# Value projection of a two-mixer decoder layer: two of its four token tiles swap PSUM banks

## The chip, the cores and the metric

The kernel runs on one core of one Trainium2 chip. The metric is device time in microseconds (us), the median of several executions. Beside it there is a trace of one profiled execution.

## The reference

One decoder layer over 1024 tokens of width 1024, in float32. A normalised input is projected eight ways; one part goes through a gated linear recurrence (RG-LRU), another through a chunked linear attention with a decaying state (HGRN2, 8 heads of width 128); gates merge both, an output projection and a residual follow, then an MLP and a last norm:

```python
proj = h @ w_in
xa, ga, q, f, v, g, m_a, m_b = jnp.split(proj, SPLIT_POINTS, axis=-1)
xa = causal_depthwise_conv(xa, conv_w, conv_b)
y_a = rg_lru(xa, w_r, b_r, w_i, b_i, lam) * jax.nn.gelu(ga)
...
o = rms_norm(hgrn2_chunkwise(qf, kf, log_f, vf), hg_norm)
y_b = o * jax.nn.silu(g)
y = jax.nn.sigmoid(m_a) * y_a + jax.nn.sigmoid(m_b) * y_b
x = x + y @ w_out
x = x + jnp.square(jax.nn.relu(rms_norm(x, norm_mlp) @ w_up)) @ w_down
return rms_norm(x, norm_final)
```

The change touches only the part `v`, the values of the linear attention.

## The kernel before

**Numbers.** Each float32 operand is split into a high part, which is a rounded copy (`split`, a ScalarE CAST at L87), and a low part, which is the rest (a VectorE subtraction at L88). Each product is then three TensorE matmuls (`mm3`, L144 to L146).

**Stages.** The mixers are worked in eight stages: 2 halves of 512 tokens (`c`) by 4 pairs of heads (`p`), stage `i` being `c, p = divmod(i, 4)`. A stage is a Python generator that yields after every few matmuls. `hgrn` for stage `i` runs on VectorE, ScalarE and GpSimd, and calls `go(n)`, which advances the generator of stage `i + 1` by `n` steps; so the projections of the next stage fill TensorE while the attention of this one is prepared. A last generator, `last_stage`, follows the eighth stage. TensorE's order is pinned to the order in which the code is written from the first stage on; the other engines' order is set by a scheduler with priorities.

**What one stage puts on TensorE, in order** (`stage`, from `i` = 2 on): the value projection of the stage before (`v_of(i)`, which calls `v_steps` for `i - 1`), the projections `xa` and `q`, most of `f`, the four gate products of the recurrence (`rg_lru`: `pr` and `pi` for `s` = 0 and `s` = 1), and the rest of `f`. Between them lie, at the places that `hgrn` chooses, the score blocks of the attention (`blocks`, L570, and the lines L690 and L701), the transposes `pk`, and the products `pkv` and `po`.

**The value projection.** `v_steps` works on four token tiles `tt` of 128 tokens. Each is a group of 24 matmuls of 256 columns into a PSUM bank of its own (tile names `pv_..._0` to `pv_..._3` in the order, `pv` in the trace), which ScalarE then copies to SBUF (L427). After the second tile (`tt` = 1; after the third in stage 2) `on_T` puts eight transposes of the previous attention's output on TensorE (`poT`, L438) into banks of another group.

**Banks.** There are eight PSUM banks in three groups (`bank`): four tagged `pj`, two `sc`, two `hg`. A new tile takes, in its group, the bank whose earlier tile is used up first in the program's order, and the first matmul into it waits for the last reader of that earlier tile. In a stage the `pj` tiles are three of the value tiles, two each of `xa`, `q` and `f`, and `pr`, `pi` for `s` = 0; the `sc` tiles are one value tile, `pr`, `pi` for `s` = 1, two score blocks and one later block of the attention (`sc64`). In the `pj` group `pr` and `pi` are opened after the two `f` tiles but are used up before them. So the value tiles that come next take the banks of `pr`, `pi`, and then of the first `f` tile, in that order.

**Who reads the `f` tiles.** `f_of` reads each of the two `f` tiles twice on ScalarE: a sigmoid into `f` (L550) and one into `kk` (L551). They stand behind `normalised` (L784, eight small ACTIVATEs that scale the attention's output) in ScalarE's queue.

Of the kernel before, what the change touches and what calls it, by code (L numbers as in the profile page):

```python
# [45 lines left out]
def trunk(ctx: ExitStack, tc: tile.TileContext, x, wts, mlp, pv, gains, mask_f, mask_u, out):  # L46
# [15 lines left out]
    def bank(tag, name):  # L62
        return ps.tile([P, 512], F32, tag=tag, name=name, bufs={"pj": 4, "sc": 2, "hg": 2}[tag])
# [68 lines left out]
    def next_w():  # L132
        used[0] += 1
        return get_w(used[0] - 1)
# [7 lines left out]
    def mm3(o, ah, al, bh, bl, first, last, goes_on=False):  # L142
        how = {"skip_group_check": True} if goes_on else {}
        pin(PE.matmul(o, ah, bh, start=first, stop=False, **how))  # L144
        pin(PE.matmul(o, ah, bl, start=False, stop=False, **how))  # L145
        pin(PE.matmul(o, al, bh, start=False, stop=last, **how))  # L146
# [49 lines left out]
    def kt(set_, k):  # L196
        return set_[0][k // 4][:, k % 4, :], set_[1][k // 4][:, k % 4, :]
# [20 lines left out]
    def mt(tag, name, shape=(P, T), dt=F32, bufs=1):  # L218
        return m.tile(list(shape), dt, tag=tag, name=name, bufs=bufs)
# [193 lines left out]
    def v_steps(c, p, got, between):  # L413
        v = mt("v", f"v_{c}{p}", (P, 4, 256))
        w = [next_w(), next_w()]
        for tt in range(4):
            pp = bank("pj" if tt < 3 else "sc", f"pv_{c}{p}_{tt}")
            for k in range(8):
                hh, hl = kt(hT[c], k)
                cut = slice(tt * P, (tt + 1) * P)  # L420
                cols = slice((k % 4) * 256, (k % 4 + 1) * 256)
                wh, wl = w[k // 4]
                mm3(pp[:, :256], hh[:, cut], hl[:, cut], wh[:, cols], wl[:, cols], k == 0, k == 7)
                if k % 2:
                    if k < 7:
                        yield
            A.copy(v[:, tt, :], pp[:, :256])  # L427
            between(tt)
            yield
        got["v"] = v  # L430
# [375 lines left out]
    def v_of(i):  # L806
        def between(tt):
            if tt == 0:
                gots[i - 1]["tail"]()
            if tt == (2 if i == 2 else 1):  # L810
                on_T(*where(i - 2), gots[i - 2])
            for n in {}.get((i, tt), ()):
                with tc.high_priority(400):
                    transposed(xn1[n], hT[1], n, f"x1{n}")

        yield from v_steps(*where(i - 1), gots[i - 1], between)

    def stage(i):
        c, p = where(i)
        got = gots[i]  # L820
        if i == 0:
            yield from v_steps(c, p, got, lambda tt: None)
        elif i > 1:
            yield from v_of(i)
# [516 lines left out]
    for part in range(2):  # L1341
# [4 lines left out]
        for hf in range(2):  # L1346
            pp = {tt: bank("pj", f"po1{hf}{tt}") for tt in tts}
# [184 lines left out]
    for kb in range(n_kb):  # L1532
        last = kb + 1 == n_kb
        qs = order[2 * kb : 2 * kb + 2]
        for half in range(2):
# [8 lines left out]
            for step, (bk, wo, uo), prs in [  # L1544
# [11 lines left out]
                for pr in prs:  # L1556
                    _, ci, cj, op = ADDS[step]
# [92 lines left out]
```

## Time and profile before

| what | value |
|---|---|
| median of 3 executions | 1545.02 us (1544.61 to 1545.60) |
| the profiled execution: from its first to its last instruction | 1544.2 us |
| busy share of that span: TensorE matmul, its weight loads, VectorE, ScalarE, GpSimd | 99%, 83%, 74%, 52%, 10% |
| mean granted TensorE clock | 0.998 of full speed |

The profiled execution's own time outside its span isn't told by the trace; the span stands 0.8 us under the median. In the trace, PE is TensorE's matmuls, PEld its weight loads, DVE is VectorE, ACT ScalarE, POOL GpSimd. A row of the chain in time gives the start in us, the duration in us, the engine, the line, the operation with output and input, and in square brackets how long the engine had stood idle before it and what ended that. The last transposes of the mixers (`poT`) start at 559.5 us; the gates, the output projection and the MLP follow.

### The profile page before, as it was taken

How to read it: one execution, taken by the hardware profiler on the slowest of the kernel's cores; microseconds unless marked ns; L12 is line 12 of the kernel's file. 1: busy time of each engine (PE TensorE's matmuls, PEld its weight loads, DVE VectorE, ACT ScalarE, POOL GpSimd, SP SyncE). 2: the span in 40 equal slices, each digit the busy share in tenths (PEclk: the TensorE clock that was granted, in tenths of full speed). 3: DMA queues.
4: the chain of work that ended last, by engine and by line, in shares of the span. 5: the costliest groups of instructions: out<-in, count | busy, mean ns of one | idle time of the engine just before them, and what ended most of it. 6: DMA issues, size and time to landing. Idle time of an engine off the chain costs nothing. (4 is left out here: it accounts for less than half of the span.)

```text
span 1544.2 us, 23190 instructions
## 1 busy us (share of the span) xinstructions
PE 1527.6 (99%) x9081; PEld 1275.3 (83%) x9081; DVE 1150.0 (74%) x1656; ACT 810.2 (52%) x1341; POOL 149.8 (10%) x188
## 2 busy tenths in 40 slices
PE   8999999999999999999999999999999999999998
PEld 7878888888888887888888888888888788888886
DVE  5798595485675928786866568888788898888877
ACT  5647757568567435453533347766666721111115
POOL 1021210233515600000000000000000000000000
PEclk9999999999999999999999999999999999999999
DMA  7555455465664274432328323666666675666642
GB/s 285 188 173 192 151 190 182 151 218 172 236 212 158 96 286 164 164 135 84 137 94 314 151 109 143 267 247 246 244 249 248 228 312 224 249 252 250 252 186 109
DMA packets 81679, 306.82 MB, mean 199 GB/s; under 512 B 8481, under 2 KB 20897, under 8 KB 68642
## 3 DMA queue, kind: packets, MB, share of 16 engines
q1 hardware_dynamic: 77536, 292.75, 51.8%
q10 hardware_dynamic: 4034, 12.59, 2.1%
q8 instruction: 71, 1.16, 0.3%
q14 instruction: 38, 0.31, 0.1%
HBM read 201.50 MB, written 103.81 MB: 198 GB/s over the span
## 5 line engine op out<-in xcount | busy, mean ns | idle before, releaser
L1559 DVE TENSOR_TENSOR acc<-acc,dX 128x512 f32<-128x512 f32 x128 | 85.0, 683 | 28.6 <-PE dX L146 26.9
L87 ACT CAST wA<-q 128x512 fp32r<-128x512 f32 x46 | 28.6, 622 | 147.5 <-PE dX L146 101.7
L88 DVE TENSOR_TENSOR wL<-raw,wH 128x1024 fp32r<-128x1024 f32 x48 | 58.8, 1225 | 46.0 <-ACT wH L87 45.7
L87 ACT CAST wH<-raw 128x1024 fp32r<-128x1024 f32 x48 | 50.4, 1050 | 39.4 <-DMA raw<-wts_in 16.1
L1559 DVE TENSOR_TENSOR acc<-acc,dY 128x512 f32<-128x512 f32 x64 | 43.4, 685 | 13.1 <-PE dY L146 12.9
L144 PE MATMUL po<-wH,y 128*128 128x512 f32 x128 | 49.8, 393 | 0.0
L145 PE MATMUL po<-wL,y 128*128 128x512 f32 x128 | 49.8, 389 | 0.0
L146 PE MATMUL po<-wH,y 128*128 128x512 f32 x128 | 49.7, 390 | 0.0
L1420 ACT ACTIVATE b<-b 128x512 f32<-128x512 f32 x48 | 30.2, 630 | 32.2 <-DVE b L1419 32.0
L88 DVE TENSOR_TENSOR wA<-q,wA 128x512 fp32r<-128x512 f32 x46 | 31.5, 686 | 16.6 <-ACT wA L87 16.4
L108 ACT CAST wH<-raw 128x1024 fp32r<-128x1024 f32 x36 | 37.7, 1048 | 9.8 <-issue 3.7
L465 DVE SCALAR_TENSOR_TENSOR xc<-xp,pvt,xc 128x512 f32<-128x512 f32 x48 | 40.1, 846 | 1.1 <-ACT xc L449 1.1
L171 POOL TENSOR_TENSOR rstd_h<-rstd_h,mhalf 128x1 f32<-128x1 f32 x8 | 4.6, 584 | 371.9 <-DVE rstd_h L166 371.9
L981 DVE TENSOR_TENSOR s<-q,q 128x512 f32<-128x512 f32 x46 | 31.6, 686 | 4.4 <-DMA q<-mlp_in 4.0
L378 POOL TENSOR_TENSOR stt<-r,stt 128x256 fp32r<-128x256 f32 x16 | 19.9, 1261 | 127.6 <-ACT stt L377 115.4
L989 DVE TENSOR_TENSOR s<-q 128x512 f32<-128x512 f32 x46 | 31.6, 686 | 0.4
L1421 ACT ACTIVATE b<-b 128x512 f32<-128x512 f32 x48 | 30.2, 631 | 1.2
L769 ACT ACTIVATE on<-po 128x128 f32<-128x128 f32 x64 | 16.9, 278 | 26.1 <-PE po L765 26.0
L1071 DVE TENSOR_TENSOR gb<-gY,ge 128x512 f32<-128x512 f32 x14 | 9.7, 690 | 25.1 <-PE gY L146 25.1
L146 PEld LDWEIGHTS po<-wH,y 128*128 128x128 f32 x128 | 24.0, 188 | 5.1
L145 PEld LDWEIGHTS po<-wL,y 128*128 128x128 f32 x128 | 24.1, 188 | 4.8
L144 PEld LDWEIGHTS po<-wH,y 128*128 128x128 f32 x128 | 24.0, 188 | 4.7
(2546 smaller groups left out, 5448.9 us busy)
## 6 DMA issues: line engine op xcount, KB each, us to landing
q<-mlp_in SPq DMA_DIRECT2D x92, 512.0 KB, 3.8
raw<-wts_in SPq DMA_DIRECT2D x80, 512.0 KB, 4.9
rest<-wL SPq DMA_DIRECT2D x36, 512.0 KB, 2.9
wL<-rest SPq DMA_DIRECT2D x36, 512.0 KB, 4.2
hd<-ri SPq DMA_DIRECT2D x16, 256.0 KB, 3.7
od<-onT ACTq DMA_DIRECT2D x8, 512.0 KB, 7.3
cdT<-stT SPq DMA_DIRECT2D x16, 256.0 KB, 3.4
o<-od SPq DMA_DIRECT2D x4, 1024.0 KB, 6.8
```

The costliest lines, as they stand in the source:

```text
L87: keep(A.copy(h, src))
L88: ins = V.tensor_tensor(out=lo, in0=src, in1=h.bitcast(F32), op=ALU.subtract)
L108: A.copy(h, raw)
L144: pin(PE.matmul(o, ah, bh, start=first, stop=False, **how))
L145: pin(PE.matmul(o, ah, bl, start=False, stop=False, **how))
L146: pin(PE.matmul(o, al, bh, start=False, stop=last, **how))
L465: ins = V.scalar_tensor_tensor(xc[:, s, :], xp[:, j : j + T], pvt[:, PV_CW + 8 * j + u : PV_CW + 8 * j + u + 1], xc[:, s, :], op0=ALU.mult ...
L981: ins = V.tensor_tensor(out=sa[:, 0, :], in0=a21, in1=a22, op=ALU.add)
L989: V.tensor_tensor(out=sb[:, 0, :], in0=a21, in1=a11, op=ALU.add)
L1420: A.activation(b[:, at, :], b[:, at, :], AF.Relu, scale=-1.0 if at == 2 else 1.0)
L1421: A.activation(b[:, at, :], b[:, at, :], AF.Square)
L1559: V.tensor_tensor(out=dst, in0=dst, in1=banks[bk, pr], op=op)
```

## The change

The third token tile (`tt` = 2) takes the bank from the `sc` group instead of the fourth one (`tt` = 3), in all eight calls of `v_steps`:

```diff
         for tt in range(4):
-            pp = bank("pj" if tt < 3 else "sc", f"pv_{c}{p}_{tt}")
+            pp = bank("sc" if tt == 2 else "pj", f"pv_{c}{p}_{tt}")
             for k in range(8):
```

The number of tiles from each group stays the same. Every engine has the same instructions in the same order before and after; what moves are the waits of three TensorE instructions in a stage. The first two places are TensorE's in stage 5, where the values of the fifth attention are projected (`poT` are the transposes of `on_T`, `pv_2` and `pv_3` the third and fourth token tile, `Activation_49` a wait for a ScalarE instruction):

```order
 L438 MATMUL poT_3498<-ident,on_3179 128x128 x3
-L144 MATMUL pv_2_3505<-wH_3288,hT10H 128x256 [waits Activation_49]
+L144 MATMUL pv_2_3505<-wH_3288,hT10H 128x256
 L145 MATMUL pv_2_3505<-wL_3289,hT10H 128x256
 L146 MATMUL pv_2_3505<-wH_3288,hT10L 128x256
@@ -1472,5 +1471,5 @@
 L145 MATMUL pv_2_3505<-wL_3310,hT11H 128x256
 L146 MATMUL pv_2_3505<-wH_3309,hT11L 128x256
-L144 MATMUL pv_3_3531<-wH_3288,hT10H 128x256
+L144 MATMUL pv_3_3531<-wH_3288,hT10H 128x256 [waits Activation_49]
 L145 MATMUL pv_3_3531<-wL_3289,hT10H 128x256
```

The wait on ScalarE moves from the first matmul of the third tile to the first matmul of the fourth, 24 matmuls later. The third place is the second bank of the `q` projection (`pj_q_1`) of the same stage, also on TensorE:

```order
 L145 MATMUL pj_q_0_3715<-hT10L,wH_3561 128x512
 L146 MATMUL pj_q_0_3715<-hT10H,wL_3562 128x512 [waits DMAHW2_49]
-L144 MATMUL pj_q_1_3716<-hT10H,wH_3561 128x512
+L144 MATMUL pj_q_1_3716<-hT10H,wH_3561 128x512 [waits Activation_49]
 L145 MATMUL pj_q_1_3716<-hT10L,wH_3561 128x512
```

It reuses the `pj` bank that the third tile held before and the fourth holds now, and has a wait on ScalarE of its own now. The second score block of the attention, which reuses the `sc` bank, waits for ScalarE in both.

## The prediction

> **What bounds the kernel now.** I read the page first, for the span and the engines' busy shares, then busy time by stretches, one for each mixer stage.
>
> ```profile
> span 1544.2 us, 23190 instructions
> PE 1527.6 (99%) x9081; PEld 1275.3 (83%) x9081; DVE 1150.0 (74%) x1656; ACT 810.2 (52%) x1341; POOL 149.8 (10%) x188
> ```
>
> ```profile
> 306.00:368.00 62.00, 61.89 (x565) 53.32 (x564) 40.54 (x69) 41.26 (x85) 24.82 (x29) 1.00 0.62 208
> 368.00:430.00 62.00, 61.89 (x565) 53.31 (x564) 40.50 (x68) 41.26 (x85) 24.82 (x29) 1.00 0.61 204
> ```
>
> The columns of the second view are the stretch, its length, the busy time of PE, PEld, DVE, ACT and POOL, the granted clock and the DMA share. In stage 5 (306 to 368 us) TensorE is idle for 0.11 us of 62; VectorE is idle for 21 and ScalarE for 21. TensorE bounds the stage, and only what stops TensorE can be worth anything. A matmul's row lasts longer than the distance to the next one, so short stops are hidden in the busy time of PE. The weight loads, PEld, show them better; so I read next who held the weight loads up, with total, number of times and longest:
>
> ```profile
> PEld sc L570 <- issue: 7.9, 23, 0.4
> PEld uX L144 <- ACT e L1416: 2.6, 7, 0.5
> PEld pv L144 <- ACT hT00H L87: 2.3, 2, 2.1
> PEld pv L144 <- ACT kk L551: 2.1, 6, 0.3
> ```
>
> The fourth row is the place of the change: six times a matmul of the value projection waits for ScalarE's `kk`, 2.1 us in all. The chain of instructions in time shows which matmul this is. First stage 5, then the same place in stage 2, and then the first and last of the six:
>
> ```profile
> 312.80 0.90 PEld L438 LDWEIGHTS poT<-ident,on 128*128 128x128 f32 x8
> 314.04 0.19 PEld L144 LDWEIGHTS pv<-wH,hT10H 128*128 128x128 f32 x1 [0.35 <-ACT kk L551]
> 314.15 0.19 PEld L145 LDWEIGHTS pv<-wL,hT10H 128*128 128x128 f32 x1
> ...
> 314.99 0.19 PEld L146 LDWEIGHTS pv<-wH,hT10L 128*128 128x128 f32 x1
> ```
>
> ```profile
> 128.07 0.90 PEld L438 LDWEIGHTS poT<-ident,on 128*128 128x128 f32 x8
> 128.94 0.19 PEld L144 LDWEIGHTS pv<-wH,hT00H 128*128 128x128 f32 x1
> ```
>
> ```profile
> 188.72 0.19 PEld L144 LDWEIGHTS pv<-wH,hT00H 128*128 128x128 f32 x1 [0.35 <-ACT kk L551]
> ```
>
> ```profile
> 498.74 0.19 PEld L144 LDWEIGHTS pv<-wH,hT10H 128*128 128x128 f32 x1 [0.35 <-ACT kk L551]
> ```
>
> In stage 5 the third value tile follows the transposes and stands still for 0.35 us. In stage 2 the transposes come one tile later, the fourth tile follows them, and there is no gap. So the gap doesn't belong to the transposes: it is the wait for the bank of the first `f` tile. ScalarE at the same place says why that bank is late:
>
> ```profile
> 304.04 0.68 ACT L491 ACTIVATE ri<-pi,pvt 128x512 f32<-128x512 f32 x1
> 304.73 1.28 ACT L491 ACT_TABLE_LOAD   x1
> ...
> 309.45 2.15 ACT L784 ACTIVATE on<-po,hrs 128x128 f32<-128x128 f32 x8
> 311.61 1.28 ACT L550 ACT_TABLE_LOAD   x1
> 312.90 0.60 ACT L550 ACTIVATE f<-pj_f 128x512 f32<-128x512 f32 x1
> 313.40 0.59 ACT L551 ACTIVATE kk<-pj_f 128x512 f32<-128x512 f32 x1
> 313.88 0.60 ACT L550 ACTIVATE f<-pj_f 128x512 f32<-128x512 f32 x1
> 314.35 0.62 ACT L551 ACTIVATE kk<-pj_f 128x512 f32<-128x512 f32 x1
> 314.83 0.40 ACT L427 COPY v<-pv 128x256 f32<-128x256 f32 x1
> ...
> 322.44 0.38 ACT L427 COPY v<-pv 128x256 f32<-128x256 f32 x1
> ...
> 322.96 0.37 ACT L427 COPY v<-pv 128x256 f32<-128x256 f32 x1
> ...
> 331.37 0.59 ACT L448 COPY xp<-pj_xa 128x512 f32<-128x512 f32 x1 [4.97 <-PE pj_xa L146]
> ```
>
> ScalarE works through its queue without a stop from 304 to 314: table loads, the eight ACTIVATEs of `on`, then the `f` tiles. The first `kk` ends at 313.40 + 0.59 = 313.99, and TensorE goes on at 314.04.
>
> **The change part by part.**
>
> *The wait that is removed.* The third tile now goes into an `sc` bank. Its earlier tile is a recurrence product for `s` = 1, and the last of those is read by the sigmoid that ends at 304.04 + 0.68 = 304.72. The transposes would let the third tile start at about 312.80 + 0.87 = 313.67 (0.87 is the distance from 128.07 to 128.94, where nothing waits). That is 9 us after the reader. So the wait is gone, not shortened.
>
> *Where the wait goes.* The fourth tile now needs the bank of the first `f` tile, free at 313.99. Weight loads of value matmuls follow each other every 0.12 us (314.15 to 314.99 are seven steps), so the 24 matmuls of the third tile take 2.9 us, and the fourth starts at 313.67 + 2.9 = 316.6. That is 2.6 us after the bank is free. Cost nothing; the 24 matmuls of the third tile are the cover. If ScalarE were over 2.6 us later, it would be back. Next in line is the second `f` tile, whose `kk` ends at 314.97; the projection `xa` waits for it and starts after the fourth tile, at 316.6 + 2.9 = 319.5.
>
> *The wait that is added.* The second bank of `q` now waits for the copy of the fourth tile (before: of the third). The fourth copy ends at 322.96 + 0.37 = 323.33. On TensorE:
>
> ```profile
> 331.94 0.75 PEld L570 LDWEIGHTS sc<-qa,kb 128*32 128x32 f32 x64 [0.35 <-issue]
> ...
> 333.33 0.19 PEld L144 LDWEIGHTS pj_q<-hT10H,wH 128*128 128x128 f32 x1
> ```
>
> `q`'s second bank begins at 333.33, 10 us after the copy: nothing, covered by the whole `xa` projection. Queued behind that matmul would be all of TensorE's later work, so the cover matters, but it is large. The second score block (331.94) reuses the `sc` bank and now waits for the third copy (322.44 + 0.38) and not for the fourth: earlier, and of no use, since neither was late. ScalarE's copies keep their order, and no DMA and no queue is moved.
>
> *What follows.* TensorE leaves the value projection earlier by the stop. Is that kept? VectorE and ScalarE wait for TensorE again soon after: the row at 331.37 shows ScalarE idle for 4.97 us until `xa` is done, and VectorE has such a row too, below. From there the stage runs as before, only sooner. One tight place remains in stage 5, which the same view shows:
>
> ```profile
> 332.90 0.44 DVE L589 COPY_PREDICATED dd<-mu,sc 128x192 f32<-128x192 uint8 x1 [2.20 <-PE sc L570]
> ...
> 351.38 0.68 DVE L560 TENSOR_TENSOR kk<-kk,seg 128x512 f32<-128x512 f32 x1
> ```
>
> ```profile
> 352.12 0.64 PEld L727 LDWEIGHTS pk<-ident,kk 128*128 128x128 f32 x6 [0.21 <-DVE kk L560]
> ```
>
> TensorE already stops for 0.21 us before `pk`, for VectorE. If VectorE's chain didn't come forward too, TensorE would wait there for the 0.35 us it gained. I take it that the chain does, as it starts from rows that wait for TensorE (332.90, 331.37).
>
> *The sum.* One stop costs the distance from the transposes to the third tile, 314.04 − 312.80 = 1.24 us, less 0.87 without a wait: 0.37 us. The row of waits gives 0.35. Six stops (stages 3 to 7 and the last generator): 2.1 to 2.2 us. Stages 0 and 2 have no such stop and gain nothing. I take 2.2: the span becomes 1544.2 − 2.2 = 1542.0. The median of the runs is 0.8 us above the span, 1545.02, so the forecast is **1542.8 us**, 0.14% less. After the mixers, other waits could take some of it:
>
> ```profile
> PEld uX L144 <- ACT e L1416: 2.6, 7, 0.5
> PEld dZ L145 <- DVE wA1230L L88: 1.0, 1, 1.0
> ```
>
> These are the largest waits after 553 us, and all are for ScalarE or VectorE, which are fed by TensorE there. They move along. A measurement of this kernel can tell about 0.2% from no change, 3.1 us; the forecast lies within that.
>
> **The rivals.**
>
> *Part is given back at `pk`.* VectorE's chain doesn't come forward in the two stages (5 and 6) whose `pk` is tight. Then 2 × 0.35 us are lost again: 1542.8 + 0.7 = 1543.5. For it: VectorE is busy for 14.1 of the 16 us before `pk`, by stretches:
>
> ```profile
> 336.00:352.00 16.00, 16.00 (x164) 13.16 (x152) 14.10 (x18) 7.75 (x11) 13.81 (x15) 1.00 0.61 204
> ```
>
> Against: it starts from a wait for TensorE of 2.20 us.
>
> *The stop was not on the path.* If something that TensorE doesn't feed (a load of weights, say) set the pace further on, the time stays at 1545.0. Against: a TensorE that is 99% busy, and no wait for a DMA among the rows above.
>
> *More than the stops.* The short stops could hold the clock down, and without them TensorE would run faster as well. What could be won is bounded by the cores' row:
>
> ```profile
> core 0: 1544.2 us, clock 0.998
> ```
>
> 0.2% of 1544.2 is 3.1 us: 1542.8 − 3.1 = 1539.7. Against: the granted clock is 1.00 in the stretches of stages 5 and 6 above, which hold stops of this kind. The Trainium skill, "TensorE: Matmul & The Clock Gate", section "A second HAM failure mode: psum-queue depth-cycling", tells of a kernel whose matmul groups cycle through PSUM banks with micro-idles between them, so often that the clock falls and rises; by that rule the time would be nearer to 1539.7. The rows speak against it here: the clock is full where the stops are.
>
> *Slower: the score bank is not free.* If the recurrence's last product for `s` = 1 (or another user of the pair) were read late, the third tile would wait there, right behind the transposes with the rest of TensorE's work behind it, and ScalarE's copies too. It decides from the point where that sigmoid ends later than 313.67, where it now ends at 304.72. A reader 1.5 us past the point would cost 6 × 1.5 = 9 us: 1545.0 − 2.2 + 9 = 1551.8. For it: ScalarE's queue is full there, and each sigmoid stands in it between casts. Against: the 9 us of margin, and that ScalarE's order isn't changed.
>
> **How the numbers follow.** The forecast 0.70; part given back 0.13; not on the path 0.08; more than the stops 0.06; slower 0.03. The forecast's own range is 1541.8 to 1543.8: the runs of before lie within 0.5 us of their median, and the later waits may add or take as much again. The range has to reach to 1543.5 and most of the way to 1545.0, and may leave out 1539.7 and 1551.8 (0.09): 1541.6 to 1544.6. Faster by over 0.2% is a time under 1541.9: the 0.06, and 0.04 of the forecast's lower end, 0.10. Slower by over 0.2%: 0.03. The rest, 0.87, is within 0.2%.
>
> **What would show it.** In the profile after, the row of `pv` waiting for `kk` is gone; `pv` follows `poT` after 0.87 us in every stage; the fourth tile, `xa` and `q`'s second bank show no gap for ScalarE; and the distance from one stage's value projection to the next is 0.35 us shorter. It is wrong if a gap of like size stands before another TensorE row of the same stage (`pk` above all), or if the stages are shorter by 2.2 us in all and the span isn't: then the place to look at is behind 553 us.

## The result and the profile after

The changed kernel takes 1542.45 us (median of 15 runs, 1541.70 to 1543.76) against 1545.03 us before (median of 15 runs, 1543.31 to 1547.24): 2.6 us less, ratio 0.9983, 95% interval 0.9976 to 0.9990. The forecast was 1542.8, with 2.2 us less.

The page of the profile after, its head:

```profile
span 1541.0 us, 23190 instructions
PE 1524.6 (99%) x9081; PEld 1273.8 (83%) x9081; DVE 1150.3 (75%) x1656; ACT 810.2 (53%) x1341; POOL 153.8 (10%) x188
```

The work of VectorE and ScalarE is the same to 0.3 us. The span is 3.2 us shorter, more than the medians differ; the part beyond the stops comes from the two ends of the program, as told further down. First the place of the change. These rows say who held up the weight loads between 150 and 560 us, before and then after (total, times, longest):

```profile
PEld sc L570 <- issue: 6.2, 18, 0.4
PEld sc L690 <- issue: 2.5, 7, 0.4
PEld pv L144 <- ACT kk L551: 2.1, 6, 0.3
PEld pk L727 <- DVE kk L560: 0.4, 2, 0.2
```

```profile
PEld sc L570 <- issue: 4.8, 14, 0.4
PEld sc L690 <- issue: 2.5, 7, 0.4
PEld sc L570 <- DVE qb L560: 1.4, 4, 0.4
PEld pk L727 <- DVE kk L560: 0.4, 2, 0.2
```

The row `pv <- ACT kk` is gone and no other row took its 2.1 us. (`sc L570` is 6.2 us before, and 4.8 + 1.4 after: the same gaps, put down to another cause in four of them.) In the chain in time of stage 5, TensorE's weight loads after:

```profile
310.50 0.90 PEld L438 LDWEIGHTS poT<-ident,on 128*128 128x128 f32 x8
311.37 0.19 PEld L144 LDWEIGHTS pv<-wH,hT10H 128*128 128x128 f32 x1
...
314.22 0.19 PEld L144 LDWEIGHTS pv<-wH,hT10H 128*128 128x128 f32 x1
...
317.10 0.19 PEld L144 LDWEIGHTS pj_xa<-hT10H,wH 128*128 128x128 f32 x1
...
330.65 0.19 PEld L144 LDWEIGHTS pj_q<-hT10H,wH 128*128 128x128 f32 x1
...
349.44 0.53 PEld L727 LDWEIGHTS pk<-ident,kk 128*128 128x128 f32 x5 [0.21 <-DVE kk L560]
```

And ScalarE at the same place after:

```profile
311.10 0.59 ACT L551 ACTIVATE kk<-pj_f 128x512 f32<-128x512 f32 x1
...
320.66 0.37 ACT L427 COPY v<-pv 128x256 f32<-128x256 f32 x1
```

The third tile follows the transposes after 0.87 us (before: 1.24), although `kk` ends only at 311.69. The fourth tile, which needs that bank now, starts at 314.22 with 2.5 us in hand; `xa` and the second bank of `q` show no gap, and the second bank of `q` comes 9.6 us after the copy that it now waits for (320.66 + 0.37 to 330.65).

From stage to stage the gain can be read without the rest of the program. The value projections of stages 5 and 6 begin, before and then after, at

```profile
306.92 0.19 PEld L144 LDWEIGHTS pv<-wH,hT10H 128*128 128x128 f32 x1
...
368.48 0.19 PEld L144 LDWEIGHTS pv<-wH,hT10H 128*128 128x128 f32 x1
```

```profile
304.62 0.19 PEld L144 LDWEIGHTS pv<-wH,hT10H 128*128 128x128 f32 x1
...
365.79 0.19 PEld L144 LDWEIGHTS pv<-wH,hT10H 128*128 128x128 f32 x1
```

This table has all such distances in us, between the first weight loads of the value projection in stages 3, 4, 5, 6, 7 and in the last generator. Each distance holds one of the six stops of before, so five of the six are in it:

| kernel | 3 to 4 | 4 to 5 | 5 to 6 | 6 to 7 | 7 to last | sum |
|---|---|---|---|---|---|---|
| before | 63.55 | 61.77 | 61.56 | 61.57 | 61.57 | 310.02 |
| after | 63.17 | 61.39 | 61.17 | 61.18 | 61.19 | 308.09 |

Every distance is 0.38 or 0.39 shorter: 1.93 us in five, so 2.3 in six if the sixth is worth as much.

### The profile page after: what moved, and what is told of

The parts are those of the page before. It is cut to its first block, busy times and chain, and to the rows that moved or that the text cites. A ratio compares the mean times of both kernels' runs of the same rounds, so it can differ in the third digit from the quotient of the medians.

```text
span 1541.0 us, 23190 instructions
## 1 busy us (share of the span) xinstructions
PE 1524.6 (99%) x9081; PEld 1273.8 (83%) x9081; DVE 1150.3 (75%) x1656; ACT 810.2 (53%) x1341; POOL 153.8 (10%) x188
```

## The experiments

Two theories stood against each other at first. The one of the prediction: six waits for the bank of the first `f` tile are gone, and that is all. And a rival that the two profiles suggest: TensorE's `xa` projection of stage 0 begins at 29.05 us before and at 27.18 after, so 1.87 of the 3.2 us were won before any of the six stops. Each kernel below was timed beside runs of its own of the kernel before; their median is 1544.50 us for the first four and 1545.31 for the other four.

**The change in the six places alone**, that is, not in stages 0 and 2:

```diff
-            pp = bank("pj" if tt < 3 else "sc", f"pv_{c}{p}_{tt}")
+            pp = bank("sc" if tt == (2 if c or p > 1 else 3) else "pj", f"pv_{c}{p}_{tt}")
```

> The change in stages 3 to 7 and the last generator alone (stages 0 and 2 as before). Theory (six waits for the bank of the first f tile, 0.37 us each, are removed and nothing else): the whole gain, 2.2 us below the kernel before, ratio 0.9986. Rival (the gain comes from the start of the program, where the two profiles differ by 1.9 us by 29 us already, or from stages 0 and 2): no change, ratio 1.000.

Measured: 1542.87 us against 1544.50, ratio 0.9992 (0.9984 to 1.0001). The interval holds both answers, so this median alone decides nothing; the trace does, for the stages. The distances from stage to stage are 63.17, 61.39, 61.19, 61.17 and 61.19: those of the changed kernel.

**The change in stages 0 and 2 alone** (the same line with 2 and 3 changed round):

> The change in stages 0 and 2 alone. Theory: no such wait stood there, so no change, ratio 1.000 within 0.0007, and six gaps of 0.35 us before the third value tile in the profile. Rival (start of the program or stages 0 and 2): 2.2 us below the kernel before, ratio 0.9986.

Measured: 1544.95 us against 1544.50, ratio 1.0003 (0.9994 to 1.0011): no change. The six waits stand where they stood:

```profile
PEld pv L144 <- ACT kk L551: 2.1, 6, 0.3
```

This kernel's profile too has an early start, `xa` at 27.28 us, and a span of 1541.3, with all six waits in place. It has the new banks in stage 0, but the start doesn't go by those: with the transposes one tile later (the next two kernels) `xa` begins at 27.87 with the old banks and at 28.47 with the new ones. An early start in one profile is not a gain of the change, and stages 0 and 2 alone give no gain in the median either: the rival is out.

**The transposes one tile later, old banks.** If the stop is a wait for a bank, it must grow when TensorE arrives sooner:

```diff
-            if tt == (2 if i == 2 else 1):
+            if tt == 2:
                 on_T(*where(i - 2), gots[i - 2])
```

> Banks as before, but the eight transposes stand behind the third value tile in every stage, not behind the second. Theory: the third tile comes 0.87 us sooner, the f bank is free no sooner, so the stop grows from 0.37 to 1.24 us in six stages: 5.2 us slower than before, ratio 1.0034. Rival (the stop is a cost of going from the transposes to the value matmuls): it moves to the fourth tile and keeps its size, ratio 1.000.

Measured: 1549.30 us against 1544.50, ratio 1.0036 (1.0022 to 1.0050). The wait, and the third tile in stage 5:

```profile
PEld pv L144 <- ACT kk L551: 7.1, 6, 1.2
```

```profile
314.50 0.19 PEld L144 LDWEIGHTS pv<-wH,hT10H 128*128 128x128 f32 x1 [1.18 <-ACT kk L551]
```

The stop is 1.18 us (1.24 expected) and stays with the third tile; the transposes, which follow a tile later, have none behind them. The rival that blames the transposes falls. The time at which the stops end says the same: in all six, here as in the kernel before, the third tile's first weight load starts 0.05 us after the first `kk` has ended.

**The transposes one tile later, new banks** (both edits):

> The changed kernel's banks and the transposes behind the third value tile in every stage. Theory: the third tile needs no f bank, the fourth comes after the transposes and finds it free: as the changed kernel, 2.2 us below the kernel before, ratio 0.9986, and over 7 us below the same order with the old banks. Rival (cost of leaving the transposes): six stops stay, ratio 1.000.

Measured: 1542.90 us against 1544.50, ratio 0.9990 (0.9981 to 0.9998), and 6.4 us below the same order with the old banks (over 7 expected). No value tile has a gap from stage 3 on. From stage 4 on the distances are those of the changed kernel (61.39, 61.19, 61.16 and 61.19). Only from stage 3 to 4 is it 0.26 longer, 63.43, and there two other transposes (`xT_x`) wait for ScalarE, 0.5 us in all. So the same edit that costs 4.8 us with the old banks costs about 0.3 us with the new ones, by the distances.

**The score bank for the second tile** (`tt == 1` in the place of `tt == 2`):

> The second value tile (and no other) takes the score bank. Theory: what counts is that three tiles, not two, stand ahead of the one that needs the f bank; the fourth tile needs it here as well. So the same gain as the changed kernel: 2.2 us below the kernel before, ratio 0.9986, no gap before a value tile from stage 3 on. Rival (the score bank must stand right behind the transposes, where a stop is worth removing for another reason): a gap of 0.35 us stays before the third tile, ratio 1.000.

Measured: 1543.10 us against 1545.31, ratio 0.9986 (0.9977 to 0.9995). No gap before a value tile, distances of 63.17, 61.39, 61.17, 61.16 and 61.19. Which of the two tiles takes the score bank doesn't matter; that three tiles stand ahead of the one that needs the `f` bank does.

**The score bank for the first tile** (`tt == 0`):

> The first value tile takes the score bank. Theory: the fourth tile needs the f bank, so the same gain, 2.2 us below the kernel before, ratio 0.9986. The first tile now needs a recurrence product for s = 1, which ScalarE reads some 2 us before the tile starts in the trace of before (304.72 against 306.92), so the margin is smaller than in the changed kernel but still there. Rival (the score bank is not free so early): a new gap before the first tile, and a part or all of the gain lost.

Measured: 1545.93 us against 1545.31, ratio 1.0004 (0.9995 to 1.0012): the whole gain is lost, against the theory's number and near the rival's, but not where the rival put it. The six waits for `kk` are gone here as well. In their place stand six others, five at `xa`, and one at the projection of the gate `g`, which follows the values in the last generator. These are the waits between 120 and 560 us, and `xa` in stage 5:

```profile
PEld pj_xa L144 <- ACT v L427: 2.7, 5, 0.5
...
PEld g L144 <- ACT v L427: 0.5, 1, 0.5
```

```profile
319.02 0.19 PEld L144 LDWEIGHTS pj_xa<-hT10H,wH 128*128 128x128 f32 x1
...
320.11 0.19 PEld L144 LDWEIGHTS pj_xa<-hT10H,wH 128*128 128x128 f32 x1 [0.54 <-ACT v L427]
```

```profile
319.69 0.37 ACT L427 COPY v<-pv 128x256 f32<-128x256 f32 x1
```

The second bank of `xa` takes the `pj` bank of the first value tile in that group. In the kernels before and after this is tile 0, copied early; here it is tile 1, whose copy stands behind a table load, the activation of `rw`, four other copies and a cast in ScalarE's queue and ends at 320.06. The theory had counted one wait, and moving every tile on by one bank moved the later ones with it. The kernel before shows how close this was, ScalarE's copy of tile 1 and then TensorE's second bank of `xa` (which there needs only the copy of tile 0), in stage 5:

```profile
320.08 0.36 ACT L427 COPY v<-pv 128x256 f32<-128x256 f32 x1
```

```profile
320.38 0.19 PEld L144 LDWEIGHTS pj_xa<-hT10H,wH 128*128 128x128 f32 x1
```

Before, TensorE came to that matmul at 320.38, and the copy of tile 1 ended at 320.44. A TensorE that comes there 0.38 us sooner and needs this copy loses the 0.38 again. So the distances of this kernel are 63.56, 61.78, 61.57, 61.57 and 61.57, those of before to 0.01. Only in stage 2 did the first tile itself wait for its score bank, as the rival said:

```profile
119.03 0.19 PEld L144 LDWEIGHTS pv<-wH,hT00H 128*128 128x128 f32 x1 [0.62 <-ACT rw L491]
```

**ScalarE later, old banks and new.** One more ScalarE instruction ahead of the sigmoids of `f`, in both kernels. It does work of no use, and what it writes is overwritten:

```diff
         kk = mt("kk", f"kk{c}{p}", (P, 2 * T))
+        twice = pp[0].unsqueeze(1).to_broadcast([P, 2, T])
+        if c or p > 1: A.activation(kk.rearrange("p (a b) -> p a b", a=2), twice, AF.Sigmoid)
```

> The kernel before with one more ScalarE instruction, a sigmoid of 128x1024 into kk that is overwritten, ahead of the first sigmoid of f in the six stages 2 to 7. It takes about 1.0 us from start to start. Theory: the bank of f is free 1.0 us later, nothing covers it, the stop before the third tile grows from 0.37 to 1.4 us: 6 us slower than before, ratio 1.004. Rival (the six stops come from something else): ratio 1.000.

Measured: 1551.10 us against 1545.31, ratio 1.0036 (1.0023 to 1.0050). ScalarE and the third tile in stage 5:

```profile
313.91 1.02 ACT L548 ACTIVATE kk<-pj_f 128x1024 f32<-128x1024 f32 x1
314.83 0.59 ACT L552 ACTIVATE f<-pj_f 128x512 f32<-128x512 f32 x1
315.31 0.60 ACT L553 ACTIVATE kk<-pj_f 128x512 f32<-128x512 f32 x1
```

```profile
315.96 0.19 PEld L144 LDWEIGHTS pv<-wH,hT10H 128*128 128x128 f32 x1 [1.26 <-ACT kk L553]
```

The extra instruction takes 0.92 us from start to start, and the stop grows by 0.91, from 0.35 to 1.26: each ScalarE microsecond ahead of `kk` is TensorE's too.

> The changed kernel with the same extra ScalarE instruction. Theory: the cover is the third tile's 24 matmuls, 2.6 us of it unused; 1.0 us later still fits, so the time stays that of the changed kernel, 2.2 us below the kernel before, ratio 0.9986. Rival (no such cover, or ScalarE's time counts by itself): as with the old banks, about 6 us over the changed kernel, ratio 1.0025.

Measured: 1543.20 us against 1545.31, ratio 0.9988 (0.9979 to 0.9997), 7.9 us below the old banks with the same extra instruction. No value tile waits, and from stage 4 on the distances are those of the changed kernel (61.39, 61.16, 61.17 and 61.19). What ScalarE's delay still costs lies elsewhere and is small: from stage 3 to 4 the distance is 0.91 longer, 64.08. Between 150 and 560 us, the waits for ScalarE and VectorE:

```profile
PEld xT_x L178 <- ACT onT L439: 1.1, 2, 0.9
PEld pk L729 <- DVE kk L562: 0.9, 3, 0.6
```

## Why the prediction was right, point by point

*TensorE is the bound, and the stop is on its path.* Shown by the two pairs: what lengthens the stop lengthens the kernel (4.8 us for six stops longer by 0.83, 5.8 us for six longer by 0.91), and with the stop gone the same two edits cost 0.3 and 0.9 us by the distances, none of it before a value tile.

*The stop is the wait for the first `f` bank.* Shown by the same pairs, by the 0.05 us between the end of `kk` and each of the stops' ends, and by the second-tile kernel, which takes the wait away by another assignment of banks.

*One stop is worth 0.37 us, six 2.2.* The distances give 0.38 to 0.39 each, 2.3 in six; the medians 2.6 (interval 1.5 to 3.7, from the ratio's), which can't tell 2.2 from 2.6. That the forecast lies 0.35 us from the measured time is thus closer than the medians can vouch for. The prediction also held that only 0.2% can be told from no change; with 15 runs each the interval was 0.07% to either side, and 0.17% stands clear of it.

*The wait moves to the fourth tile and is covered there.* Right: 2.5 us in hand, 2.6 forecast. An extra 0.92 us of ScalarE fitted in. That the stop would come back past the 2.5 us was not tried.

*The added wait of `q` costs nothing.* Right: 9.6 us in hand.

*The score bank is free for the third tile.* Right: `pv` follows `poT` after 0.86 or 0.87 us from stage 3 on. In stage 2 it follows after 1.26, but for another reason, told below. The score bank can be late: with the first tile in it, stage 2 waited 0.62 us.

*VectorE's chain comes forward with TensorE, so nothing is given back at `pk`.* Right. The gap before `pk` in stages 5 and 6 is 0.21 us before and after. VectorE's wait for TensorE, from which its chain starts, was 2.20 us in stage 5 and is 1.83 after. It is shorter by 0.37, as TensorE comes sooner, and the rest of it is still there:

```profile
330.21 0.45 DVE L589 COPY_PREDICATED dd<-mu,sc 128x192 f32<-128x192 uint8 x1 [1.83 <-PE sc L570]
```

*More than the stops, through the clock.* No sign of it: the mean granted clock was 0.998 of full speed before and is 0.999 after, 1.00 in the stretches of stages 5 and 6 in both, and the distances fell by the stops and no more.

*The step from the span to the median* was mis-sized, without harm. The prediction set the time outside the span at 0.8 us, which mixed one execution's span with the median of others. The runs that have both give 1.8 us (the changed kernel's profiled run: 1542.76 and 1541.0). The profiled execution of before was thus about 1 us slower than its median. As the 0.8 was first the difference of the two and then added back, it dropped out of the forecast.

*Why the spans differ by 3.2 us.* Of that, 1.87 us were won by 29 us, where the wait for the first normalised tokens was 2.3 us before and 0.7 after:

```profile
PEld pv L144 <- ACT hT00H L87: 0.7, 2, 0.5
```

This wait differs from kernel to kernel without regard to the banks: in two kernels whose stage 0 is as before it is 2.2 us (six places) and 1.4 (late `f`, old banks). Against it stand 0.4 us in stage 2, where a TensorE that came early waited for ScalarE's `on` (the six-places kernel, whose stage 2 is as before, stops there as well: 1.23 us from the first transpose to the tile behind them in the place of 0.87), and 0.6 us behind the mixers, one wait of the MLP above all:

```profile
PEld dY L146 <- DVE u15t L88: 1.8, 1, 1.8
```

It was 0.6 us before. Both ends vary by about 2 us over the ten profiles: `xa` begins between 27.18 and 29.05 us, and from the first weight load behind the last transposes (`gX`) to the end it takes 983.2 to 985.4. That the runs of one kernel differ in the same places would fit the spread of their times; it isn't shown, as each kernel has one profile.

## What to carry to other kernels

When a matmul waits for a PSUM bank, look for who reads the bank's earlier tile and whether another group has a bank that is already free; one swap can put a whole tile's matmuls between the reader and the next user (here 24 matmuls, 2.9 us). A swap can give later tiles of that group other banks, so follow the ring to its end and hold each new pair of reader and user against the trace: here the same swap with the first tile took the six stops away and put as much back at the next projection. With an effect near the spread of runs, the distance between two equal places of the program shows what the median of the whole can't.

## What the runs showed that was not expected

The tile that should get the spare bank was thought to be of no matter as long as the `f` bank came last. It mattered: second or third, 0.9986 and 0.9983; first, 1.0004. ScalarE's copies of tiles 0 and 1 start 5 us apart (314.83 and 320.08 in the trace of before), though a tile's matmuls take only 2.9 us, and only tile 0's copy is early enough for `xa`.
